# Expert 0's tokens by one-hot products, a joint mask selector, and value products in the array's column halves

## The chip, the cores and the metric

One core of a Trainium2 chip runs one program. The time is the device time of one execution in microseconds (us); the figure compared is the median of the runs. A trace of one execution was taken with the hardware profiler. The engines are TensorE (PE in the rows, with PEld for its weight loads), VectorE (DVE), ScalarE (ACT), GpSimd (POOL) and SyncE (SP), which issues the large transfers.

## The reference

Two transformer blocks on 512 tokens of 1024 columns, in fp32. What matters here:

```python
# first block, SSD mixer: 4 groups of 3 heads, chunks of 128 tokens
lmat = exp(where(causal, a_cs[..., :, None] - a_cs[..., None, :], -inf))
y_diag = einsum('bcgls,bcghls,bcsghp->bclghp', cb, lmat, xdt)
# second block, forgetting attention: 8 heads of 64, query blocks of 128
logits = q @ k.T / sqrt(d) + (cum[t] - cum[s]);  p = softmax(masked logits)
o = p @ v                      # then rms_norm per head
# second block, mixture of experts: 16 experts, two per token
h = h + concat(o_a, o_b) @ w_out
t = rms_norm(h, ffn_norm)
gates = ...                    # top-1 group, top-2 experts in it
for e in range(16):
    y += gates[:, e] * ((silu(t @ w_gate[e]) * (t @ w_up[e])) @ w_down[e])
out = rms_norm(h + y, final_norm)
```

## The kernel before

A scheduler places the instructions of the whole program on the engines; waits come from its semaphores, `issue_after` adds an order by hand. All weights stream from HBM by SP's queue in units of 512 KB (`fill`, line 212, tile `raw`), are split into a high part on ScalarE (`whi`, line 270) and a low part on VectorE, or by a plan on GpSimd (`wlo`, line 271), and go into rings of five. `mm3` (lines 276 to 278) multiplies hi by hi, lo by hi and hi by lo: three matmuls of 512 columns for a product of fp32 quality. A plain fp32 matmul runs as two passes, which the trace shows as two instructions.

*SSD mask.* For each of 4 chunks and 4 groups one unit (`ssd_mask_unit`) makes three heads' differences of cumulative sums in PSUM: the causal mask (line 840), then a selector times the sums' high part (841) and low part (842), 48 partitions each, then the group's products (843).

*Forgetting attention.* For each query block tt and head: q by k (1532), mask (1533), row maximum, exp on ScalarE (1536), transposes of p (`tr`, 1540), a copy `fox_pT` (1543 or 1545), the value product with pT stationary and v's 64 columns moving (1548), and a scale by the row sum's reciprocal on VectorE (1550). Other matmuls of projections fill the gaps.

*Start of the MoE.* The last projection (`projR` over `w_out_2`) adds its result to x per token tile tt (line 403) and calls `after(tt)`: transposes of x (`tr`, 2023), routing logits (2028), the normed rows to HBM (`xnd`), ranks by matmuls (1731, 1732) and a one-hot of expert 0's slots (`rt_oh`, 2049). Once the last tile's rank is known, `slots_row` (1833 to 1841) makes the row numbers of the 96 slots of experts 0 and 1, two indirect transfers on POOL's queue fetch these tokens from `xnd` (`ex_g`, 1874), PE transposes them (1887), and `put_split` (315) makes `ex_xh` and `ex_xl`, the moving side of expert 0's gate and up products. Later experts' rows come from `route`, whose small operations VectorE does at this start. A 4-byte-per-slot transfer `mark` on SP's queue (2116) holds back the weight loads behind it until the row numbers of expert 0 exist. The final norm's gain is brought as one row and spread over the partitions by PE (125, 126).

Of the kernel before, what the change touches and what calls it, by code (L numbers as in the profile page):

```python
# [70 lines left out]
class Kern:  # L71
# [306 lines left out]
    def projR(s, src, ld, nk, get, x, after, tail=3, mid=None, lag=2, order=None):  # L378
# [4 lines left out]
        for half in range(2):  # L383
            cs = slice(half * 512, half * 512 + 512)
# [391 lines left out]
    def ssd_dt(s, pd, x):  # L776
# [725 lines left out]
    def fox_main(s, pool, qa, ka, v, on):  # L1502
# [21 lines left out]
        for tt in range(NT):  # L1524
# [5 lines left out]
            for h in range(8):  # L1530
                ps = s.psm.tile([P, 512], F32, name="sm")
                nc.tensor.matmul(ps[:, :n], qa[:, h, sl], ka[:, h, :n], start=True, stop=False)  # L1532
                nc.tensor.matmul(ps[:, tt * P:n], s.identb, s.neg_gt, start=False, stop=True)
                V.tensor_reduce(nm[:, h:h + 1], ps[:, :n], AX.X, OP.max, negate=True)
                p = pool.tile([P, T], F32, name="fox_p", bufs=2)
                nc.scalar.activation(p[:, :n], ps[:, :n], AF.Exp, bias=nm[:, h:h + 1], accum_out=sm[:, h:h + 1])
                yield
                pt = s.ptr.tile([P, 512], F32, name="tr")
                for j in range(tt + 1):
                    nc.tensor.transpose(pt[:, j * P:j * P + P], p[:, j * P:j * P + P], s.ident)  # L1540
                pT = pool.tile([P, T], F32, name="fox_pT", bufs=2)
                if h % 2:
                    V.tensor_copy(pT[:, :n], pt[:, :n])
# [436 lines left out]
    def moe(s, mixT):  # L1980
# [70 lines left out]
        def after(tt):  # L2051
# [276 lines left out]
```

## Time and profile before

| | us |
|---|---|
| median of 3 runs | 1455.51 (1454.84 to 1457.64) |
| the profiled execution | 1453.98 |
| its span in the trace | 1452.2 |
| TensorE busy in it | 1399.7 |

The span runs from the first to the last instruction of the trace; the profiled execution's own time is 1.8 us longer. Mean granted clock of TensorE is 0.987 of full speed.

### The profile page before, as it was taken

Reading aid. Unit: us, or ns where it says so; the run is one execution under the profiler, and the core shown is the slowest. Engines: PE = TensorE matmul, PEld = TensorE weight load, DVE = VectorE, ACT = ScalarE, POOL = GpSimd, SP = SyncE. Lnnn points to the kernel's source line nnn. Section 1 sums busy time; section 2 is a strip of 40 time slices with the busy share of each in tenths; the row PEclk is TensorE's granted clock in tenths of the full one; section 3 lists DMA queues with packets and bytes.
Section 4 is the critical chain, followed back from the end, with each engine's and each line's share of the span. In section 5 each row is a group of like instructions: output and inputs, shape, how many; then the busy total and the mean of one; then the engine's idle time right before and its main releaser. Section 6 shows DMA issues by size and latency. Waiting matters only on the chain.

```text
span 1452.2 us, 20178 instructions
## 1 busy us (share of the span) xinstructions
PE 1399.7 (96%) x7467; PEld 1130.2 (78%) x7467; DVE 977.7 (67%) x1772; ACT 779.2 (54%) x1200; POOL 103.8 (7%) x103
## 2 busy tenths in 40 slices
PE   7999999999999999999999999999998599999996
PEld 6888887787879888888888889877887367777774
DVE  6989577565465444444365997766555599999997
ACT  6465654434334333233344685554443388888885
POOL 1000000010010000000000400000102111111111
PEclk9999999999999999999999999999999699999998
DMA  7353342521223333323232423120754899999993
GB/s 199 92 136 112 90 131 73 174 88 58 75 71 116 102 95 94 101 88 100 89 101 87 134 74 88 41 77 18 260 204 172 226 357 356 353 343 349 349 349 130
DMA packets 145933, 223.51 MB, mean 154 GB/s; under 512 B 18466, under 2 KB 71106, under 8 KB 145816
## 3 DMA queue, kind: packets, MB, share of 16 engines
q1 hardware_dynamic: 136852, 200.48, 42.7%
q0 software_dynamic: 3568, 10.34, 3.0%
q10 hardware_dynamic: 5412, 11.37, 2.2%
q8 instruction: 59, 0.97, 0.3%
q14 instruction: 42, 0.34, 0.1%
HBM read 208.41 MB, written 14.95 MB: 154 GB/s over the span
## 4 chain that ended last, share of the span: by engine, by line
PE 86%; DVE 6%; ACT 3%; DMA 2%; issue 2%; POOL 1%; DVEq 0%; SPq 0%; ACTq 0%; POOLq 0%
PE mm L276 24%; PE mm L278 24%; PE mm L277 24%; PE sm L1416 2%; PE tr L1548 1%; PE tr L323 1%; PE tr L1887 1%; PE sm L1532 1%; POOL rs_r L291 1%; DMA ex_g<-xnd,sn_i 1%; DVE wlo L271 1%; PE sm L879 1%; PE sm L276 1%; PE tr L1540 1%; PE sm L2028 1%
## 5 line engine op out<-in xcount | busy, mean ns | idle before, releaser
L271 DVE TENSOR_TENSOR wlo<-raw,whi 128x1024 fp32r<-128x1024 f32 (+1 forms) x351 | 423.6, 1222 | 216.4 <-ACT whi L270 213.5
L270 ACT ACTIVATE whi<-raw 128x1024 fp32r<-128x1024 f32 (+1 forms) x356 | 372.7, 1057 | 293.2 <-PE mm L277 154.0
L276 PE MATMUL mm<-hT_hi,whi 128*128 128x512 f32 (+1 forms) x768 | 283.2, 369 | 1.9 <-DVE x L403 1.7
L278 PE MATMUL mm<-hT_hi,wlo 128*128 128x512 f32 (+1 forms) x768 | 281.5, 367 | 0.0
L277 PE MATMUL mm<-hT_lo,whi 128*128 128x512 f32 (+1 forms) x768 | 280.9, 366 | 0.0
L276 PE MATMUL mm<-whi,hT_hi 128*128 128x512 f32 (+1 forms) x592 | 219.7, 371 | 1.4 <-ACT hT_hi L315 1.4
L278 PE MATMUL mm<-whi,hT_lo 128*128 128x512 f32 (+1 forms) x592 | 217.9, 368 | 0.0
L277 PE MATMUL mm<-wlo,hT_hi 128*128 128x512 f32 (+1 forms) x592 | 217.0, 367 | 0.0
L278 PEld LDWEIGHTS mm<-hT_hi,wlo 128*128 128x128 f32 x768 | 144.7, 188 | 24.3
L276 PEld LDWEIGHTS mm<-hT_hi,whi 128*128 128x128 f32 x768 | 144.3, 188 | 24.8 <-DVE x L403 1.9
L277 PEld LDWEIGHTS mm<-hT_lo,whi 128*128 128x128 f32 x768 | 144.6, 188 | 23.3
L276 PEld LDWEIGHTS mm<-whi,hT_hi 128*128 128x128 f32 x592 | 111.8, 189 | 20.7 <-ACT hT_hi L315 2.3
L278 PEld LDWEIGHTS mm<-whi,hT_lo 128*128 128x128 f32 x592 | 111.7, 189 | 19.2 <-issue 0.6
L277 PEld LDWEIGHTS mm<-wlo,hT_hi 128*128 128x128 f32 x592 | 112.0, 189 | 18.5 <-issue 1.0
L276 PE MATMUL mm<-whi,ex_xh 128*96 128x512 f32 x256 | 102.8, 402 | 1.3 <-ACT ex_xh L315 0.6
L291 POOL TENSOR_TENSOR rs_r<-rs_v,mhalf 128x1 f32<-128x1 f32 (+2 forms) x42 | 33.4, 798 | 980.2 <-DVE rs_v L289 823.9
L277 PE MATMUL mm<-wlo,ex_xh 128*96 128x512 f32 x256 | 101.4, 396 | 0.0
L278 PE MATMUL mm<-whi,ex_xl 128*96 128x512 f32 x256 | 100.9, 395 | 0.0
L276 PEld LDWEIGHTS mm<-whi,ex_xh 128*96 128x96 f32 x256 | 41.5, 162 | 19.0 <-ACT ex_xh L315 1.1
L278 PEld LDWEIGHTS mm<-whi,ex_xl 128*96 128x96 f32 x256 | 41.6, 162 | 18.1
L277 PEld LDWEIGHTS mm<-wlo,ex_xh 128*96 128x96 f32 x256 | 41.8, 163 | 16.9
L1246 DVE SCALAR_TENSOR_TENSOR cv<-mm,cols,cv 128x511 f32<-128x511 f32 (+1 forms) x44 | 33.0, 749 | 30.0 <-ACT cv L1243 29.2
(568 smaller groups left out, 2060.3 us busy)
## 6 DMA issues: line engine op xcount, KB each, us to landing
raw<-in_w_gate SPq DMA_DIRECT2D x64, 512.0 KB
raw<-in_w_up SPq DMA_DIRECT2D x64, 512.0 KB
raw<-in_w_down SPq DMA_DIRECT2D x64, 512.0 KB
raw<-in_ffn_w_up SPq DMA_DIRECT2D x44, 512.0 KB
raw<-in_w_in SPq DMA_DIRECT2D x40, 512.0 KB
raw<-in_ffn_w_down SPq DMA_DIRECT2D x22, 512.0 KB
raw<-in_w_out SPq DMA_DIRECT2D x16, 512.0 KB
raw<-in_w_in SPq DMA_DIRECT2D x8, 520.0 KB
```

The costliest lines, as they stand in the source:

```text
L270: s.hi_op = s.nc.scalar.activation(hv, v, AF.Copy).ins
L271: eng.tensor_sub(lv, v, hv.bitcast(F32))
L276: mm(ps, a.hi[asl], b.hi[bsl], start=first, stop=False)
L277: mm(ps, a.hi[asl], b.lo[bsl], start=False, stop=False)
L278: mm(ps, a.lo[asl], b.hi[bsl], start=False, stop=last)
L291: s.pow_op = nc.gpsimd.tensor_tensor(r, v, s.mhalf[:, :n], OP.pow).ins
L323: nc.tensor.transpose(ps[:, i * P:(i + 1) * P], src[:, (k0 + i) * P:(k0 + i + 1) * P], s.ident)
L879: nc.tensor.matmul(yd[:, o:o + 64], L[:, j], xdt[:, h], start=True, stop=True)
L1246: V.scalar_tensor_tensor(y[:, d:], ps[:, :512 - d], cw[:, w:w + 1], y[:, d:], op0=OP.mult, op1=OP.add)
L1416: nc.tensor.matmul(ps[:, sl], qk[:, sl], qk[:, sl], start=True, stop=True)
L1532: nc.tensor.matmul(ps[:, :n], qa[:, h, sl], ka[:, h, :n], start=True, stop=False)
L1540: nc.tensor.transpose(pt[:, j * P:j * P + P], p[:, j * P:j * P + P], s.ident)
```

## The change

Three parts. (1) The SSD mask's sums are stacked, high parts in partitions 0 to 47 and low parts in 64 to 111, so that one matmul over 128 partitions stands where two over 48 stood; the stacking takes a memset and copies once. (2) In the forgetting attention v is stationary (128 by 64) and pT moves 128 columns; two heads' results go to PSUM partitions 0 to 63 and 64 to 127. The pair is copied by ScalarE (`fox_oT`), transposed back by PE and scaled by one VectorE operation. (3) Expert 0's tokens are not fetched: `first(tt)` multiplies chunks of x (stationary) by a one-hot (now fp32, `rt_oh0`) into two PSUM tiles, and 8 ScalarE and 8 VectorE operations make `ex_xh` and `ex_xl` with the norm's gain. `mark` and expert 0's gather go; two early splits move from GpSimd to VectorE; the final gain comes as one 512 KB transfer on POOL's queue; expert 1's row numbers are made on VectorE alone, and its transposes are ordered after the third unit of expert 0's up product.

```diff
--- before
+++ after
@@ -381,6 +381,7 @@
+            adds = s.add_ops = []
@@ -400,7 +401,7 @@
-                nc.vector.tensor_add(x[:, tt, cs], x[:, tt, cs], pss[tt])
+                adds.append(nc.vector.tensor_add(x[:, tt, cs], x[:, tt, cs], pss[tt]).ins)
@@ -806,26 +807,34 @@
...
+        c2 = s.tmp.tile([P, P], F32, name="ssd_c2", tag="h")
+        V.memset(c2, 0.0)
+        for r in (0, 64):
+            V.tensor_copy(c2[:, r:r + 48], cs[:, 0].rearrange("p a b -> p (a b)"))
         pt = s.ptr.tile([P, 512], F32, name="tr")
-        nc.tensor.transpose(pt[:48, 0:P], cs[:, 0].rearrange("p a b -> p (a b)"), s.ident)
-        hl = s.tmp.tile([48, 2, P], F32R, name="ssd_hl", tag="h")
-        hi, lo = hl[:, 0], hl[:, 1]
-        s.put_split(pt[:48, 0:P], hi, lo)
-        s.ssd_cs = Split(*(pd.tile([48, 3, P], F32R, name="ssd_c" + i) for i in ("H", "L")))
-        sh = [48, 3, P]
-        for o, v in ((s.ssd_cs.hi, hi), (s.ssd_cs.lo, lo)):
-            V.tensor_mul(o, v.bitcast(F32)[:, None, :].to_broadcast(sh), hm[:, :, None].to_broadcast(sh))
+        nc.tensor.transpose(pt[:, 0:P], c2, s.ident)
+        hl = s.tmp.tile([P, 2, P], F32R, name="ssd_hl", tag="h")
+        nc.scalar.activation(hl[:, 0], pt[:, 0:P], AF.Copy)
+        V.tensor_sub(hl[:, 1], pt[:, 0:P], hl[:, 0].bitcast(F32))
+        s.ssd_cs = pd.tile([P, 3, P], F32R, name="ssd_cH")
+        sh = [64, 3, P]
+        for i in range(2):
+            r = slice(64 * i, 64 * i + 64)
+            V.tensor_mul(s.ssd_cs[r], hl[r, i].bitcast(F32)[:, None, :].to_broadcast(sh), hm[r, :, None].to_broadcast(sh))
         yield
@@ -836,10 +845,9 @@
-        sel = s.ssd_sel[:, u:u + 1].to_broadcast([48, P])
...
-        nc.tensor.matmul(o, sel, s.ssd_cs.hi.rearrange("p j t -> p (j t)"), start=False, stop=False)
-        nc.tensor.matmul(o, sel, s.ssd_cs.lo.rearrange("p j t -> p (j t)"), start=False, stop=True)
+        nc.tensor.matmul(o, s.ssd_sel[:, u:u + 1].to_broadcast([P, P]), s.ssd_cs.rearrange("p j t -> p (j t)"),
+                         start=False, stop=True)
@@ -1527,27 +1535,40 @@
-            for h in range(8):
...
+            for h0 in range(0, 8, 2):
+                pTs = []
+                for h in (h0, h0 + 1):
...
+                    yield
+                    pt = s.ptr.tile([P, 512], F32, name="tr")
...
+                    pTs.append(pT)
+                V.reciprocal(ri[:, h0:h0 + 2], sm[:, h0:h0 + 2])
+                for j in range(tt + 1):
+                    for i in range(2):
+                        nc.tensor.matmul(pt[i * 64:i * 64 + 64, 0:P], v[:, j, (h0 + i) * 64:(h0 + i) * 64 + 64],
+                                         pTs[i][:, j * P:j * P + P], start=j == 0, stop=j == tt)
+                oT = pool.tile([P, P], F32, name="fox_oT", bufs=2)
+                nc.scalar.activation(oT, pt[:, 0:P], AF.Copy)
+                next(rest, None)
                 yield
-                pt = s.ptr.tile([P, 512], F32, name="tr")
...
-                V.reciprocal(ri[:, h:h + 1], sm[:, h:h + 1])
-                for j in range(tt + 1):
-                    nc.tensor.matmul(pt[:, 0:64], pT[:, j * P:j * P + P], v[:, j, h * 64:h * 64 + 64],
-                                     start=j == 0, stop=j == tt)
-                V.tensor_scalar_mul(on[:, tt, h * 64:h * 64 + 64], pt[:, 0:64], ri[:, h:h + 1])
+                nc.tensor.transpose(pt[:, P:2 * P], oT, s.ident)
+                hs = slice(h0 * 64, h0 * 64 + P)
+                V.tensor_mul(on[:, tt, hs].rearrange("p (h d) -> p h d", h=2),
+                             pt[:, P:2 * P].rearrange("p (h d) -> p h d", h=2),
+                             ri[:, h0:h0 + 2, None].to_broadcast([P, 2, 64]))
                 next(rest, None)
@@ -1795,8 +1816,9 @@
-        V.tensor_tensor(oh, s.slot[:, None, :].to_broadcast([P, 8, CAP]),
-                        rk.rearrange("p i t -> p (i t)")[:, :, None].to_broadcast([P, 8, CAP]), OP.is_equal)
+        with s.tc.issue_after(s.row_op):
+            V.tensor_tensor(oh, s.slot[:, None, :].to_broadcast([P, 8, CAP]),
+                            rk.rearrange("p i t -> p (i t)")[:, :, None].to_broadcast([P, 8, CAP]), OP.is_equal)
@@ -1833,12 +1855,8 @@
         ix = pool.tile([CAP, 1], I32, name=f"sn_i{e}")
-        if e:
-            nc.scalar.activation(v, ps[:CAP, 0:2], AF.Copy)
-        else:
-            nc.vector.tensor_copy(v, ps[:CAP, 0:2])
-        eng = nc.gpsimd if e else nc.vector
-        s.row_op = eng.tensor_scalar(ix, v[:, 0:1], v[:, 1:2], float(T), op0=OP.add, op1=OP.add).ins
+        nc.vector.tensor_copy(v, ps[:CAP, 0:2])
+        s.row_op = nc.vector.tensor_scalar(ix, v[:, 0:1], v[:, 1:2], float(T), op0=OP.add, op1=OP.add).ins
         return ix
@@ -1894,12 +1912,17 @@
             for k in range(2):
-                s.mm3(ps[:CAP], xT, (slice(None), k0 + k), w, (slice(None), k), k0 + k == 0, k0 + k == 7)
+                op = s.mm3(ps[:CAP], xT, (slice(None), k0 + k), w, (slice(None), k), k0 + k == 0, k0 + k == 7)
+            if k0 == 4:
+                s.gate_op = op
         return ps
+    def expert_xT(s, pool):
+        return Split(pool.tile([P, KD, CAP], F32R, name="ex_xh", bufs=1),
+                     pool.tile([P, KD, CAP], F32R, name="ex_xl", bufs=1))
     def expert_pick(s, pool, xg):
-        xT = Split(pool.tile([P, KD, CAP], F32R, name="ex_xh", bufs=1),
-                   pool.tile([P, KD, CAP], F32R, name="ex_xl", bufs=1))
+        xT = s.expert_xT(pool)
         s.pick(xg, lambda k0, ps: s.put_split(ps, xT.hi[:, k0:k0 + 4], xT.lo[:, k0:k0 + 4]))
@@ -2013,7 +2036,16 @@
         s.rr = pr.tile([P, NT], F32, name="rt_r")
-        oh = pr.tile([P, NT, CAP], BF16, name="rt_oh")
+        oh = [pr.tile([P, NT, CAP], (F32, BF16)[e], name=f"rt_oh{e}") for e in range(2)]
+        p0 = []
+        def first(tt):
+            for b in range(2):
+                for k in range(4):
+                    c = (4 * b + k) * P
+                    nc.tensor.matmul(p0[b][:, k * CAP:(k + 1) * CAP], x[:, tt, c:c + P], oh[0][:, tt],
+                                     start=tt == 0 and k == 0, stop=tt == 3 and k == 3)
@@ -2046,7 +2078,8 @@
             s.route_rank(tt, pl[:, 160 + tt * 16:176 + tt * 16])
-            V.tensor_scalar(oh[:, tt], s.slot, s.rk[:, tt, 0:1], None, op0=OP.is_equal)
+            for e in range(2):
+                V.tensor_scalar(oh[e][:, tt], s.slot, s.rk[:, tt, e:e + 1], None, op0=OP.is_equal)
@@ -2058,6 +2091,10 @@
                     ranks(tt - 1)
+            if tt == 3:
+                p0.extend(s.pmm.tile([P, 512], F32, name="mm") for _ in range(2))
+                for i in range(3):
+                    first(i)
             V.scalar_tensor_tensor(la[:, tt], pl[:, tt * 20:tt * 20 + 20], r, s.rb, op0=OP.mult, op1=OP.add)
@@ -2074,7 +2111,11 @@
         s.projR("w_out_2", D, KD, lambda half, k: mixT, x, after, mid=mid, lag=0, order=(4, 6, 0, 2), tail=3)
+        gf = s.gain.tile([P, D], F32, name="gain")
+        with s.tc.issue_after(s.pow_op):
+            nc.gpsimd.dma_start(gf, dap(A["final_norm_2"], 0, [[0, P], [1, D]]))
         ranks(3)
+        first(3)
@@ -2084,39 +2125,30 @@
-        hi_op = None
-        s.plan = [(nc.gpsimd, []), (nc.gpsimd, [s.pow_op])]
+        s.plan = [(V, [s.add_ops[0]]), (V, [s.add_ops[1]])]
+        late, s.late = s.late, 1000
         s.fill(most=L3, splits=2)
-        hi_op = s.hi_op
+        s.late = late
-        ix = []
-        for e in range(XG):
-            if e:
-                oh = pn.tile([P, NT, CAP], BF16, name="sn_oh")
-                sh = [P, NT, CAP]
-                V.tensor_tensor(oh, s.slot[:, None, :].to_broadcast(sh), s.rk[:, :, e:e + 1].to_broadcast(sh), OP.is_equal)
-            with s.tc.issue_after(s.rank_op):
-                ix.append(s.slots_row(pn, e, oh))
-            s.gather(xgs[e], ix[e])
-            if not e:
-                s.fence = [s.row_op]
-        grow = s.tmp.tile([1, D], F32, name="grow", tag="h", bufs=1)
-        with s.tc.issue_after(hi_op):
-            nc.scalar.dma_start(grow, dap(A["final_norm_2"], 0, [[D, 1], [1, D]]))
-        with s.tc.issue_after(s.logit_op), s.tc.issue_after(hi_op):
-            gf = s.bcast_pe(s.gain, grow, "gain")
+        with s.tc.issue_after(s.rank_op):
+            ix1 = s.slots_row(pn, 1, oh[1])
+        s.gather(xgs[1], ix1)
         for tt in range(AL, NT):
...
         s.rings["raw"] = [s.pool(f"raw4_{i}", ctx=c3, side="right") for i in range(N4)] + s.rings["raw"]
-        mark = s.dram.tile([CAP, 1], I32, name="mark")
-        with s.tc.issue_after(nc.sync.dma_start(mark, ix[0]).ins):
-            s.fill()
+        s.fence = [s.row_op]
+        s.fill()
         s.late = FL[5]
-        xT = s.expert_pick(pe, xgs[0])
+        xT = s.expert_xT(pe)
+        for k in range(KD):
+            ps = p0[k // 4][:, k % 4 * CAP:k % 4 * CAP + CAP]
+            gk = s.cols2[:, 96 + k:97 + k]
+            nc.scalar.activation(xT.hi[:, k], ps, AF.Copy, scale=gk)
+            V.scalar_tensor_tensor(xT.lo[:, k], ps, gk, xT.hi[:, k].bitcast(F32), op0=OP.mult, op1=OP.subtract)
         s.route(pr, pe, lgg, lge)
@@ -2159,7 +2191,8 @@
             pu = s.expert_gate(pe, e, xT, "w_up_2")
-            xT = s.expert_pick(pe, xgs[(e + 1) % XG])
+            with s.tc.issue_after(s.gate_op) if e == 0 else nullcontext():
+                xT = s.expert_pick(pe, xgs[(e + 1) % XG])
             if e:
```

On TensorE, from the last tile's transposes on, these rows stood ahead of expert 0 before (`rt_o` a matrix of ones, `grow` the final gain's row, `ex_g_9992` expert 0's tokens, `ex_xh` and `whi` the first expert product):

```order
L1748 LDWEIGHTS rt_o
L1748 MATMUL sm<-rt_Mb,rt_o 128x16
L125 MATMUL mm<-grow,ones 128x512 x2
L1887 MATMUL tr<-ident,ex_g_9992 128x96 x8
L276 MATMUL mm<-whi,ex_xh 96x512
L277 MATMUL mm<-wlo,ex_xh 96x512
L276 MATMUL mm<-whi,ex_xh 96x512
```

In the changed kernel the products of `first` begin right behind the projection's last matmuls, on both sides of the last tile's transposes (2055 is the old line 2023, 2060 the old 2028):

```order
L277 MATMUL mm<-wlo,hT_hi 128x512
L278 MATMUL mm<-whi,hT_lo 128x512
L2047 MATMUL mm<-rt_oh_9484,x 128x96 x15
L2055 MATMUL tr<-ident,x 128x128 x4
L2047 MATMUL mm<-rt_oh_9484,x 128x96
L2060 MATMUL sm<-rt_w,rt_h 128x20 x4
L1752 LDWEIGHTS rt_o
```

The last eight of `first` stand directly ahead of expert 0, with the small matmuls of expert 1's row numbers (1855):

```order
L1769 MATMUL sm<-rt_Mb,rt_o 128x16
L2047 MATMUL mm<-rt_oh_9484,x 128x96 x8
L1855 LDWEIGHTS rt_oh_9485
L1855 MATMUL sm<-rt_tb,rt_oh_9485 96x2
L276 MATMUL mm<-whi,ex_xh 96x512
L277 MATMUL mm<-wlo,ex_xh 96x512
L278 MATMUL mm<-whi,ex_xl 96x512
```

So expert 0 now stands behind `first(3)` and not behind a transfer, line 125 is gone, and 15 products of `first` stand ahead of the last tile's transposes. Expert 1's eight transposes stand after all of expert 0's gate and up products, as before.

On VectorE, before, this piece of the route's work ended ahead of expert 0's two `ex_xl`:

```order
L271 TENSOR_TENSOR wlo<-raw,whi 128x1024
L1772 TENSOR_TENSOR rt_M_10146<-rt_M,rt_w 128x128
L1782 TENSOR_TENSOR rt_y_10148<-rt_tb,rt_M 128x64x2
L1784 TENSOR_TENSOR rt_y_10148<-rt_M,rt_r 128x64
L1782 TENSOR_TENSOR rt_y_10148<-rt_tb,rt_M 128x64x2
L1784 TENSOR_TENSOR rt_y_10148<-rt_M,rt_r 128x64
L1786 COPY rt_y_10148<-rt_M_10146 128x128
L1798 TENSOR_TENSOR rt_y_10149<-rt_s,rt_rk_10159 128x768
L315 TENSOR_TENSOR ex_xl<-tr,ex_xh 128x384 x2
```

In the changed kernel the same stretch has eight smaller `ex_xl` mixed with the route's operations and a weight split (`wlo`):

```order
L2151 SCALAR_TENSOR_TENSOR ex_xl<-mm,cols_2799,ex_xh 128x96 x2
L1789 TENSOR_TENSOR rt_w<-rt_w,rt_se 128x4
L1818 TENSOR_REDUCE rt_rk_10181<-rt_x 128x4
L2151 SCALAR_TENSOR_TENSOR ex_xl<-mm,cols_2799,ex_xh 128x96 x2
L1790 RECIPROCAL rt_w<-rt_w 128x4
L1817 TENSOR_TENSOR rt_x<-rt_M,rt_rk 128x64
L1791 TENSOR_TENSOR rt_w<-rt_w,rt_e_10155 128x4
L271 TENSOR_TENSOR wlo<-raw,whi 128x1024
L2151 SCALAR_TENSOR_TENSOR ex_xl<-mm,cols_2799,ex_xh 128x96 x2
L1793 TENSOR_TENSOR rt_M_10168<-rt_M,rt_w 128x128
```

What stood ahead of expert 0's splits now stands among and behind them.

In the attention's last query block, TensorE before (`fox_v` and `fox_pT` in the value product, each of four rows two passes):

```order
L1540 MATMUL tr<-ident,fox_p 128x128 x4
L277 MATMUL mm<-wlo,hT_hi 128x512
L278 MATMUL mm<-whi,hT_lo 128x512
L1540 MATMUL tr<-ident,fox_p 128x128 x4
L1548 MATMUL tr<-fox_v,fox_pT 128x64 x4
L276 MATMUL mm<-whi,hT_hi 128x512
L277 MATMUL mm<-wlo,hT_hi 128x512
```

and in the changed kernel, where two heads' products stand in one row and the transpose of `fox_oT` follows behind two matmuls of a projection:

```order
L1561 MATMUL tr<-fox_pT,fox_v 64x128 x8
L276 MATMUL mm<-whi,hT_hi 128x512
L277 MATMUL mm<-wlo,hT_hi 128x512
L1567 MATMUL tr<-ident,fox_oT 128x128
L1550 MATMUL tr<-ident,fox_p 128x128 x4
L1542 MATMUL sm<-fox_k,fox_q 128x512
L1550 MATMUL tr<-ident,fox_p 128x128 x4
```

Two value products of 64 columns became a pair of 128 columns, with one transpose more for the pair.

## Rows read from the trace of the kernel before

**Rows 1.** Page, part 4: the chain that ended last, by engine
```profile
PE 86%; DVE 6%; ACT 3%; DMA 2%; issue 2%; POOL 1%; DVEq 0%; SPq 0%; ACTq 0%; POOLq 0%
```

**Rows 2.** Stretches: length; busy us of PE, PEld, DVE, ACT, POOL; PEclk, DMA share, GB/s
```profile
955.00:1025.00 70.00, 69.26 (x414) 52.71 (x413) 42.88 (x132) 32.55 (x83) 6.59 (x4) 1.00 0.16 46
...
1130.00:1146.60 16.60, 5.57 (x20) 2.67 (x18) 5.21 (x24) 3.00 (x6) 3.42 (x3) 0.50 0.92 165
1146.60:1161.20 14.60, 13.95 (x67) 9.53 (x66) 10.31 (x19) 9.97 (x12) 1.79 (x2) 0.90 0.85 287
1180.00:1280.00 100.00, 100.00 (x476) 70.99 (x475) 91.99 (x91) 86.11 (x102) 14.56 (x11) 1.00 1.04 356
1410.00:1420.00 10.00, 10.00 (x47) 7.04 (x46) 8.91 (x9) 8.72 (x10) 1.57 (x1) 1.00 0.73 234
```

**Rows 3.** Timeline of PE at the MoE's start: start, us, operation, idle before
```profile
1121.43 0.66 PE L2023 MATMUL tr<-ident,x 128*128 128x128 f32 x4 [2.54 <-DVE x L403]
...
1129.23 0.24 PE L1833 MATMUL sm<-rt_tb,rt_oh 128*96 128x2 bf16 x1 [0.34 <-DVE rt_oh L2049]
...
1145.10 1.54 PE L1887 MATMUL tr<-ident,ex_g 96*128 96x96 f32 x8 [11.03 <-DMA ex_g<-xnd,sn_i]
1146.62 0.74 PE L276 MATMUL mm<-whi,ex_xh 128*96 128x512 f32 x1
```

**Rows 4.** The chain over the same stretch: start, us
```profile
1118.70 1.75 DVE rt_oh L2049
...
1124.87 1.32 DVE rs_t L301
1130.83 14.23 DMA ex_g<-xnd,sn_i
```

**Rows 5.** Timeline of VectorE: the same one-hot later, and the last splits
```profile
1128.92 0.26 DVE L2049 TENSOR_SCALAR rt_oh<-rt_s,rt_rk 128x96 bf16<-128x96 f32 x1
...
1429.06 2.36 DVE L271 TENSOR_TENSOR wlo<-raw,whi 128x1024 fp32r<-128x1024 f32 x2 [0.20 <-ACT whi L270]
```

**Rows 6.** Timeline of POOL: a weight split
```profile
1118.03 2.35 POOL L271 TENSOR_TENSOR wlo<-raw,whi 128x1024 fp32r<-128x1024 f32 x1 [1.13 <-ACT whi L270]
```

**Rows 7.** Timeline of PE: one SSD mask unit
```profile
184.20 0.43 PE L841 MATMUL sm<-ssd_cH,ssd_sel 48*128 48x384 f32 x1
184.48 0.34 PE L842 MATMUL sm<-ssd_cL,ssd_sel 48*128 48x384 f32 x1
```

**Rows 8.** Timeline of PE in the forgetting attention
```profile
1000.11 0.60 PE L1540 MATMUL tr<-ident,fox_p 128*128 128x128 f32 x4
1000.55 1.02 PE L1532 MATMUL sm<-fox_k,fox_q 66*128 66x512 f32 x2
1001.46 1.10 PE L1548 MATMUL tr<-fox_v,fox_pT 128*128 128x64 f32 x8
1002.40 0.22 PE L1533 MATMUL sm<-neg_gt,identb 128*128 128x128 bf16 x1
```

**Rows 9.** Lines 1548 and 1545 over the span: ns min/median/max, first and last start
```profile
L1548 PE MATMUL tr<-fox_v,fox_pT x160: 217/275/323, 949.0 to 1020.1; 128*128 128x64 f32 x160
...
L1545 ACT ACTIVATE fox_pT<-tr x16: 277/428/598, 948.7 to 1017.2; 128x128 f32<-128x128 f32 x4, 128x256 f32<-128x256 f32 x4, 128x384 f32<-128x384 f32 x4, 128x512 f32<-128x512 f32 x4
```

**Rows 10.** Timeline of PE: S5's products in the array's column halves
```profile
105.39 0.39 PE L277 MATMUL mm<-hT_lo,whi 128*128 128x512 f32 x1
105.63 0.40 PE L278 MATMUL mm<-hT_hi,wlo 128*128 128x512 f32 x1
105.95 2.09 PE L686 MATMUL sm<-s_U,s_I 128*64 128x64 f32 x64
107.97 0.55 PE L695 MATMUL sm<-s_U,s_T 128*128 128x64 f32 x3
```

**Rows 11.** Tile ex_g: its gathers from issue to landing
```profile
DMA to landing us min/median/max: 8.4/11.4/14.4
```

**Rows 12.** Page, part 5: ScalarE's weight splits, mean ns of one
```profile
L270 ACT ACTIVATE whi<-raw 128x1024 fp32r<-128x1024 f32 (+1 forms) x356 | 372.7, 1057 | 293.2 <-PE mm L277 154.0
```

More of the change, by code (lines that the diff above doesn't have):

```diff
@@ L277, in mm3 @@
         mm(ps, a.hi[asl], b.lo[bsl], start=False, stop=False)
-        mm(ps, a.lo[asl], b.hi[bsl], start=False, stop=last)
+        return mm(ps, a.lo[asl], b.hi[bsl], start=False, stop=last).ins
     def rstd(s, ss, n, width, pool, v0=None, out=None):
@@ L807, in ssd_dt @@
         yield
-        it = s.tmp.tile([48, 16], F32, name="ssd_it", tag="h")
-        nc.gpsimd.iota(it, pattern=[[-3, 16]], base=0, channel_multiplier=1, allow_small_or_imprecise_dtypes=True)
-        eq = s.tmp.tile([48, 4, 16], F32, name="ssd_eq", tag="h")
+        it = s.tmp.tile([P, 16], F32, name="ssd_it", tag="h")
+        for r in (0, 64):
+            nc.gpsimd.iota(it[r:r + 64], pattern=[[-3, 16]], base=0, channel_multiplier=1,
+                           allow_small_or_imprecise_dtypes=True)
+        eq = s.tmp.tile([P, 4, 16], F32, name="ssd_eq", tag="h")
         for j in range(3):
@@ L1529, in fox_main @@
             ri = s.stat.tile([P, 8], F32, name="fox_ri")
-            for h in range(8):
[L1531 to L1536, printed above, removed]
-                yield
-                pt = s.ptr.tile([P, 512], F32, name="tr")
-                for j in range(tt + 1):
[L1540 to L1543, printed above, removed]
-                else:
-                    nc.scalar.activation(pT[:, :n], pt[:, :n], AF.Copy)
-                V.reciprocal(ri[:, h:h + 1], sm[:, h:h + 1])
-                for j in range(tt + 1):
-                    nc.tensor.matmul(pt[:, 0:64], pT[:, j * P:j * P + P], v[:, j, h * 64:h * 64 + 64],
-                                     start=j == 0, stop=j == tt)
-                V.tensor_scalar_mul(on[:, tt, h * 64:h * 64 + 64], pt[:, 0:64], ri[:, h:h + 1])
@@ new lines, in fox_main @@
+            for h0 in range(0, 8, 2):
+                pTs = []
+                for h in (h0, h0 + 1):
+                    ps = s.psm.tile([P, 512], F32, name="sm")
+                    nc.tensor.matmul(ps[:, :n], qa[:, h, sl], ka[:, h, :n], start=True, stop=False)
+                    nc.tensor.matmul(ps[:, tt * P:n], s.identb, s.neg_gt, start=False, stop=True)
+                    V.tensor_reduce(nm[:, h:h + 1], ps[:, :n], AX.X, OP.max, negate=True)
+                    p = pool.tile([P, T], F32, name="fox_p", bufs=2)
+                    nc.scalar.activation(p[:, :n], ps[:, :n], AF.Exp, bias=nm[:, h:h + 1], accum_out=sm[:, h:h + 1])
+                    yield
+                    pt = s.ptr.tile([P, 512], F32, name="tr")
+                    for j in range(tt + 1):
+                        nc.tensor.transpose(pt[:, j * P:j * P + P], p[:, j * P:j * P + P], s.ident)
+                    pT = pool.tile([P, T], F32, name="fox_pT", bufs=3)
+                    if h % 2:
+                        V.tensor_copy(pT[:, :n], pt[:, :n])
+                    else:
+                        nc.scalar.activation(pT[:, :n], pt[:, :n], AF.Copy)
+                    pTs.append(pT)
+                V.reciprocal(ri[:, h0:h0 + 2], sm[:, h0:h0 + 2])
+                for j in range(tt + 1):
+                    for i in range(2):
[4 more added lines that the diff above has]
+                next(rest, None)
+                yield
+                nc.tensor.transpose(pt[:, P:2 * P], oT, s.ident)
[3 more added lines that the diff above has]
+                             ri[:, h0:h0 + 2, None].to_broadcast([P, 2, 64]))
```

6 lines of the change are left out of this document (3 added, 3 removed).

## The prediction

> **What bounds the kernel now.** I read the chain that ended last first: TensorE holds 86% of it [rows 1]. Then the stretches [rows 2]: in the attention's, 955 to 1025, TensorE is busy 69.3 of 70 us, and among the experts, 1180 to 1280, 100 of 100. There an instruction taken off TensorE is worth its slot, from its start to the next one's, and work added on other engines costs nothing until one of them is full. VectorE is near that among the experts (92 of 100 us), and the DMA engines too (share 1.04, 356 GB/s). The one large hole is the MoE's start: between 1130 and 1146.6 TensorE does 5.6 us of work. Its timeline shows why [rows 3]: a wait of 2.54 us for the last tile of x, the last one-hot used at 1129.23, and then 11.03 us of idling until expert 0's tokens land; the first expert product starts at 1146.62. The chain names three pieces there [rows 4]: a one-hot of 1.75 us, a small operation of 1.32 us, the transfer of 14.23 us. The clock granted is 0.50, the lower level, from 1130 to 1146.6, and 0.90 on the mean of the next 14.6 us [rows 2]: after idling the engine works at half speed for a while, and 0.10 of 14.6 us is 1.5 us lost.
>
> **SSD mask.** Line 841 takes .28 us, to the start of line 842 [rows 7], which is of the same form. One matmul of the same 384 columns over 128 partitions replaces both. How long it takes over more partitions no row shows for this form; a 512-column product over 128 partitions takes .24 to the next one [rows 10], so nothing speaks for more than .28. One slot of some .27 goes, in 16 units: −4.3 us. The stacking's memset and two copies are some .5 us of VectorE work, once, in a mixer that TensorE fills; if bare, +.5.
>
> **Value products.** 8 passes took 1001.46 to 1002.40, .1175 each [rows 8]; there are 160 [rows 9], so 18.8 us. The new form also has 160 passes (80 products, two each), each of 128 columns over half the array, the halves in turn. The nearest row is S5's: 64 passes of 64 columns into column halves took 105.95 to 107.97, .0316 each [rows 10]; twice the columns gives .063, 10.1 us in all. If the halves did not overlap, a pass of 128 columns would take what a transpose of 128 does, .44 / 4 = .11 [rows 8], 17.6 in all. I take .063, since that row has this very form of output. To it come 16 transposes of `fox_oT` at .11, 1.8 us. Going into the halves cost .09 there (.32 for the product ahead against .24 for the one before), coming out I put at .11; at 16 pairs 3.2 us. And the new path, value product, ScalarE copy, transpose, needs cover: ScalarE's copy of 128 columns takes .28 us [rows 9], with the two hand-overs I estimate .6, and the new order puts two to five other matmuls of .23 us in between, .46 us and up. In half the pairs I count .1 to .2 us bare, 1 us in all. Sum: −18.8 + 10.1 + 1.8 + 3.2 + 1 = −2.7; as some of the old waits already lay in the 18.8, I take −2. Bounds −6 (no price for the halves, all covered) and +5 (halves not overlapped).
>
> The Trainium skill, TensorEngine Tiling (Array Packing), section Key Properties, says that a change of tiling mode drains TensorE, which speaks against this part. The product ahead of S5's row has .40 us of duration and left after .32 [rows 10], so what stands there is no full drain; were each of 32 changes a drain at .40 − .24 = .16 us, it would be 5.1 us in place of 3.2, and this part would come to about 0.
>
> **Start of the MoE.** Where the last one-hot was used at 1129.23 [rows 3], the changed order gives: the one-hot that holds the chain for 1.75 us [rows 4] while GpSimd splits a weight (1118.03 for 2.35 us [rows 6]) takes .26 elsewhere [rows 5], −1.5; the 1.32 us operation on a column of 128 values [rows 4], which should take no more than that either, −1.1; the last tile's transposes stand behind 15 products of `first`, of two passes each at about .1175 [rows 8], 3.5 us from 1118.7, when the 2.54 us wait began, so they start at 1122.2 and not 1121.43 [rows 3], +.75; two splits that move to VectorE (2.36 us for two [rows 5]), mostly in a pause, +.5. Together the last one-hot at about 1127.9. `first(3)` is 8 × .23 = 1.85 us, a ScalarE copy of a quarter tile .3: expert 0 starts at about 1130.0 and not at 1146.62, −16.6. If TensorE stays at full clock there (it has 7.4 us of new products in the old pauses), −1.5 as well. The matmuls of line 125, last ahead of expert 0's transposes, lay under the gather's wait and give nothing more.
>
> Against it stands VectorE's work, for which the wait was the cover. From 1130 to 1161.2, when expert 1 starts, it did 5.21 + 10.31 = 15.5 us [rows 2]: route, `ex_xl`, weight splits. TensorE's work on expert 0 is 48 products of .23 to .24 and some small ones, 11.5 us. Queued behind the route's operations on VectorE are the splits of up's units, for which TensorE waits. So VectorE is 4.0 us too late, at most; with 8 small `ex_xl` for 2 large ones about as much is added as the new order does earlier. I take the whole 4.0, since nothing else then limits. Sum −16.6 − 1.5 + 4.0 = −14. Bounds: −18 (VectorE keeps up: the splits ahead in the ring suffice) and −8 (expert 1 late too, below).
>
> **The sum** is −4.3 − 2 − 14 = −20.3 against the profiled execution's 1453.98, so 1433.7; the median lies 1.5 above that execution, so **1435**.
>
> **The rivals.**
> *Expert 1's tokens are late* (0.10). Its gather is issued after `first(3)`, at about 1131.2, and gathers took 8.4 to 14.4 us to land [rows 11]: 1139.6 to 1145.6. Expert 1 wants them at 1141.5, or 1145.5 if VectorE is late. For it: the weight loads that `mark` held back (165 GB/s in 1130 to 1146.6 against 356 later [rows 2]) now run beside it. Against it: later gathers ran beside the full stream, and only one now stands where two did. Price 3 to 6 us more: 1438 to 1441.
> The Trainium skill, SBUF — State Buffer, section SBUF: two separate sides, says that a transfer issued from GpSimd cannot write its descriptors while VectorE holds their shared port; VectorE will be full when this one is issued. The range of landings above already includes those with VectorE at 92%.
>
> *The weight stream becomes the bound* (0.10). TensorE gains 14 us here, the stream only what its hole gives: (1 − 165/356) × 16.6 = 8.9 us at most, less 1.4 for the 512 KB of the final gain. Its margin at the end: the transfers end near 1417 (share .73 of 1410 to 1420 [rows 2]), the last two splits begin at 1429.06 [rows 5], with 1.06 of ScalarE's part ahead [rows 12] some 11 us of margin. 14 − 7.5 = 6.5 would be eaten, 4.5 left. If the hole does not close, 14 eats all of it and 3 us more: 1438.
>
> *More than I sum* (0.13). VectorE is hidden (−4) or the attention's part reaches its bound (−4): 1427 to 1431.
>
> *Slower* (0.04). The attention's pair path is bare: TensorE waits in each of 16 pairs until ScalarE, behind one weight split of 1.06 us [rows 12] and another operation of that kind, copies `fox_oT`. It decides above (20.3 − 1) / 16 = 1.2 us bare in each pair beside what I counted; with two operations ahead, 2.1 + .6 − .5 of cover = 2.2 us, it is +34 against −20, and 1469 or so; with one ahead, 1.2, no change. Against it: ScalarE is busy 32.6 of 70 us there [rows 2], so it is free more often than not when the pair ends.
>
> *The change does not do what it says* (0.03): another wait of the start takes the gather's place (the 8 ScalarE and VectorE operations, or `first(3)`, behind late splits), and the attention eats the mask's gain: 1453 to 1457.
>
> **How the numbers follow.** My forecast, 1429 to 1441, has 0.60. With the late gather, the stream and part of the larger gain the range 1427 to 1445 leaves out the rest, under 2 in 10. A change of 0.2%, 2.9 us, is about what a measurement of this kernel tells from none. Faster: 0.60 + 0.10 + 0.10 + 0.13 = 0.93; within 0.2%: 0.03; slower: 0.04.
>
> **What would show it.** Right: the slot of the joint selector at .24 to .28 and one a unit; pairs of value passes at .06 each and little idling ahead of the `fox_oT` transposes; expert 0's first product some 17 us nearer to the last product of w_out, at full clock; TensorE idling 3 to 5 us within expert 0 and before expert 1, for `wlo` or `ex_xl`. Wrong: passes at .11; waits for `fox_oT` over .5 us in most pairs; expert 1's transposes waiting for `ex_g`; waits for `raw` near the end.

## The result and the profile after

The changed kernel takes 1431.21 us (median of 4, 1429.26 to 1432.94) against 1455.32: ratio 0.9831, 95% interval 0.9813 to 0.9849, 24.1 us faster. 1435 was forecast, in 1427 to 1445. The profiled execution took 1432.94, the slowest of the four; its span is 1431.2, 21.0 below that of before. Where these went, from the starts of TensorE's first or last product of each kind in the two traces:

| from, to | before | after | change |
|---|---|---|---|
| start, first mask unit | 173.75 | 174.88 | +1.1 |
| first mask unit, cross attention's first product (SSD) | 147.83 | 138.81 | −9.0 |
| to the attention's first `fox_q` product | 622.12 | 623.58 | +1.5 |
| to the first `hg_v` product behind the attention | 80.49 | 78.57 | −1.9 |
| to the last product of w_out | 94.31 | 94.28 | 0.0 |
| to expert 0's first product | 28.12 | 13.91 | −14.2 |
| to expert 0's first down product (`ex_hh`) | 27.60 | 28.57 | +1.0 |
| to the end | 277.98 | 278.60 | +.6 |

The rows of untouched code move as much between executions that share that code: the first took 173.75 to 175.43 us in four (before, e7, e3, e4; the stacking is not in them), the third 622.1 to 623.6 us in the same four. The +.6 at the end stands in every kernel with the new start (278.5 to 278.6 us against 277.9 to 278.1); where it comes from stays open.

One mask unit, first of before (the two lines of [rows 7] stand between these), then of after:

```profile
183.94 0.33 PE L840 MATMUL sm<-neg_lt,identb 128*128 128x384 bf16 x1
...
184.99 0.36 PE L276 MATMUL mm<-memT_hi,whi 128*128 128x256 f32 x1
```

```profile
183.96 0.33 PE L848 MATMUL sm<-neg_lt,identb 128*128 128x384 bf16 x1
183.98 0.48 PE L849 MATMUL sm<-ssd_cH,ssd_sel 128*128 128x384 f32 x1
184.30 0.38 PE L851 MATMUL sm<-CT,BT 128*128 128x128 f32 x2
184.44 0.36 PE L277 MATMUL mm<-memT_lo,whi 128*128 128x256 f32 x1
```

To the next product it took 1.05 us, now .48. All 16 units are alike, 1.045 us on the mean before and .481 after. That is .57 off in place of the .27 that I counted: besides the second selector product, the rows around it shrank. The mask ahead of the selector (840, now 848) went from .26 to .03 to the next start, and the group's products (843, now 851) from .25 to .14.

In the attention, one group of the last query block, and what TensorE waited for over the stage (us in total, times, longest):

```profile
994.97 1.09 PE L1561 MATMUL tr<-fox_pT,fox_v 128*64 128x128 f32 x16
996.00 0.23 PE L1543 MATMUL sm<-neg_gt,identb 128*128 128x128 bf16 x1
```

```profile
PE tr L1561 <- DVE fox_pT L1553: 1.7, 3, 0.6
PE tr L1567 <- ACT fox_oT L1564: 1.0, 1, 1.0
```

16 passes take 1.03 us to the start of the next product, .064 each; over the stage 160 passes take 11.2 us where 17.3 stood. The shorter groups are dearer by the pass: groups of 4, 8, 12 and 16 take .37, .59, .81 and 1.03 us, which is .055 a pass and .15 for each group. The groups of before have no such part (8 passes .81 to .94, .117 a pass by a line through all groups). Waits went from .6 to 2.7 us.

The MoE's start, the timeline of TensorE and the stretches (columns as in [rows 2]):

```profile
1110.35 3.48 PE L2047 MATMUL mm<-rt_oh,x 128*128 128x96 f32 x30
1113.67 0.60 PE L2055 MATMUL tr<-ident,x 128*128 128x128 f32 x4
...
1116.69 3.07 PE L2047 MATMUL mm<-rt_oh,x 128*128 128x96 f32 x16 [0.60 <-DVE rt_oh L2082]
...
1120.44 3.73 PE L2047 MATMUL mm<-rt_oh,x 128*128 128x96 f32 x16
...
1124.03 0.72 PE L276 MATMUL mm<-whi,ex_xh 128*96 128x512 f32 x1
...
1128.69 0.47 PE L276 MATMUL mm<-whi,ex_xh 128*96 128x512 f32 x1 [0.46 <-ACT ex_xh L2150]
...
1138.05 0.82 PE L1905 MATMUL tr<-ident,ex_g 96*128 96x96 f32 x8
1140.35 0.47 PE L276 MATMUL mm<-whi,ex_xh 128*96 128x512 f32 x1 [1.48 <-ACT ex_xh L315]
```

```profile
1110.12:1124.03 13.91, 12.72 (x93) 12.25 (x92) 9.35 (x57) 4.20 (x8) 1.15 (x2) 0.76 1.01 350
1124.03:1127.60 3.57, 3.57 (x11) 2.37 (x10) 3.08 (x14) 1.39 (x5) 1.06 (x1) 0.50 0.90 297
1127.60:1141.00 13.40, 11.46 (x61) 7.63 (x59) 11.90 (x29) 11.02 (x15) 4.16 (x1) 1.00 1.00 341
1160.00:1360.00 200.00, 200.00 (x950) 142.00 (x949) 184.00 (x180) 171.93 (x204) 29.29 (x23) 1.00 1.04 352
```

Expert 0 starts 13.9 us behind w_out where it was 28.1. No wait there names VectorE beyond the .60 for a one-hot, nor the gather of expert 1. But the granted clock is 0.50, the lower level, from 1117.4, within the first stretch, to 1127.7: `first(2)` and `first(3)`, of 16 passes each, take 2.87 and 3.52 us to the next row, the 30 passes ahead 3.32. Before expert 1 the wait is 1.48 for `ex_xh`. From 1160 on TensorE is gapless as before, and TensorE never waits for the weight stream, at 352 GB/s.

The profiled execution of a second measurement of the same kernel (e0_after, below) has a span of 1428.6 us, with 13.6 us to expert 0 and 27.5 from there to `ex_hh`: there the clock was at 0.50 for 6.8 us of this start, here for 10.2.

### The profile page after: what moved, and what is told of

Its sections match the earlier page's. It is cut to its first block, busy times and chain, and to the rows that moved or that the text cites. A ratio compares the mean times of both kernels' runs of the same rounds, so it can differ in the third digit from the quotient of the medians.

```text
span 1431.2 us, 20262 instructions
## 1 busy us (share of the span) xinstructions
PE 1393.5 (97%) x7515; PEld 1129.9 (79%) x7515; DVE 972.1 (68%) x1754; ACT 779.1 (54%) x1218; POOL 98.9 (7%) x101
## 4 chain that ended last, share of the span: by engine, by line
PE 71%; DVE 3%; ACT 1%; issue 1%; POOL 1%; DMA 0%; DVEq 0%; POOLq 0%; ACTq 0%; SPq 0%
PE mm L276 20%; PE mm L278 20%; PE mm L277 20%; PE sm L1424 2%; PE tr L1905 1%; PE sm L1542 1%; POOL rs_r L291 1%; PE mm L2047 1%; PE sm L276 1%; PE tr L1561 1%; PE sm L278 1%; PE tr L323 1%; PE sm L277 1%; PE sm L2060 0%; PE tr L1550 0%
## 5 line engine op out<-in xcount | busy, mean ns | idle before, releaser
L278 PEld LDWEIGHTS mm<-whi,hT_lo 128*128 128x128 f32 x592 | 112.3, 190 | 18.8 <-issue 0.8
```

Source lines behind the costliest of these rows:

```text
L278: return mm(ps, a.lo[asl], b.hi[bsl], start=False, stop=last).ins
```

## The experiments

All ratios are to the kernel before.

**e1_ssd, e3_fox, e4_moe: each part alone**, the other hunks of the diff left out.

> Only the joint mask selector, the rest as before. If the matmul's own slot is what it saves (my prediction's term): 16 x .27 = 4.3 us off 1455.3, 1451.0. If going from products over 128 partitions to products over 48 and back costs about .2 us each way, which the joint selector removes too: 16 x (.17 + .2 + .2) less some .08 that the next product gives back, 6 to 8 us off, 1447.5 to 1449.5.

Measured: 1447.60, ratio 0.9943 (0.9930 to 0.9956), −8.3 us. The second case of its expectation, steps between 128 and 48 partitions.

> Only the attention's value products in the column halves, the rest as before. My prediction's term: -2 us, 1453.3. If the attention alone is worth nothing (passes cheaper, but steps into and out of the halves, transposes and waits eat it): 1455.3 within 1 us. The profile should show passes of about .07 and the product behind each group of them some .1 us later than elsewhere.

Measured: 1453.06, ratio 0.9983 (0.9974 to 0.9991), −2.5 us by the ratio: my term, and clear of no change, though only by a little.

> Only the start of the MoE by one-hot products, the rest as before. My prediction's term: -14 us, 1441.3. From the changed kernel's trace, where the offset to before goes from -8.4 at the last projection's end to -21.2 in the experts: -12.8, 1442.5. If the three parts help each other (the start finds other buffers free than alone): less than 12, over 1443.5.

Measured: 1442.84, ratio 0.9909 (0.9896 to 0.9922), −13.2 us. The three ratios multiply to 0.9836; the parts add up, and no help of one to another shows.

**e2_ssd_two: is it the number of selector products, or their 48 partitions?** On e1:

```diff
-        nc.tensor.matmul(o, s.ssd_sel[:, u:u + 1].to_broadcast([P, P]), s.ssd_cs.rearrange("p j t -> p (j t)"),
-                         start=False, stop=True)
+        for r in range(2):
+            nc.tensor.matmul(o, s.ssd_sel[:, r, u:u + 1].to_broadcast([P, P]), s.ssd_cs.rearrange("p j t -> p (j t)"),
+                             start=False, stop=r == 1)
```

> The stacked sums of the joint selector, but still two selector matmuls a unit, each over all 128 partitions with a selector that is zero in the other half. If a matmul's slot is the cost: no change to before, 1455 (+.5 for the added VectorE work). If the step between 48 and 128 partitions is the cost: the two slots shrink to about .17 each and the steps are gone, 16 x .4 less .08 x 16 is some 4 to 5 us off, 1450 to 1452, and the mask ahead of them takes .03 instead of .26 start to start.

Measured: 1449.89, ratio 0.9960 (0.9948 to 0.9973), −5.8 us with as many products as before. Its timeline of TensorE, one unit:

```profile
188.09 0.33 PE L851 MATMUL sm<-neg_lt,identb 128*128 128x384 bf16 x1
188.12 0.65 PE L853 MATMUL sm<-ssd_cH,ssd_sel 128*128 128x384 f32 x2
188.60 0.38 PE L855 MATMUL sm<-CT,BT 128*128 128x128 f32 x2
188.74 0.36 PE L277 MATMUL mm<-memT_lo,whi 128*128 128x256 f32 x1
```

.65 to the next product: .40 less than before's 1.05, with the mask at .03 and two selector products in .48; the 16 units are alike, .654 on the mean. So two steps between 128 and 48 partitions cost .40 us a unit, 6.4 in 16 units, and the second product the rest, .17 a unit. The Trainium skill, TensorEngine Tiling (Array Packing), section Key Properties, says that a change of tiling mode drains TensorE; these rows agree with it if a product over 48 partitions counts as such a change, which no run here shows by itself. I had not looked for it in this part of the change. For the column halves the rows show .15 us a group (above and e11).

**e5_fox_serial: do the halves have to alternate?** The loop over the pair's two heads stands outside that over j.

> The changed kernel (1431.2), with the value products of a pair in the order first all of one head, then all of the other, so that the column halves no longer alternate. If the halves overlap only when they alternate: the passes go from .07 to about .11, 160 x .04 = 6.4 us more, 1437 to 1438. If half an array's columns are cheaper in any order: .07 as before, 1431.

Measured: 1433.46, ratio 0.9837 (0.9823 to 0.9852), by its time not separable from the changed kernel. Its timeline, the same group as above:

```profile
996.03 1.58 PE L1561 MATMUL tr<-fox_pT,fox_v 128*64 128x128 f32 x16
997.54 0.23 PE L1543 MATMUL sm<-neg_gt,identb 128*128 128x128 bf16 x1
```

1.51 us for 16 passes, .094 each, against .064: here alternating saves a third. But groups of 4 and 8 take .37 and .59 us in either order; only those of 12 and 16 are longer, by .27 and .49 us. So the order counts where six or eight passes of one half stand in a row, and not where two or four do. Over the stage the passes take 14.2 us for 11.2, the stage 80.8 us for 78.6. Neither number of the expectation: a pass in one half alone is not the .11 of a whole array's 128 columns.

**e6_fox_wide: no column halves.** Per j one product with both heads' v stationary, 128 columns, and both pT moving:

```diff
-                    for i in range(2):
-                        nc.tensor.matmul(pt[i * 64:i * 64 + 64, 0:P], v[:, j, (h0 + i) * 64:(h0 + i) * 64 + 64],
-                                         pTs[i][:, j * P:j * P + P], start=j == 0, stop=j == tt)
...
+                    nc.tensor.matmul(pt[:, 0:2 * P], v[:, j, h0 * 64:h0 * 64 + P], pT[:, j].rearrange("p i t -> p (i t)"),
+                                     start=j == 0, stop=j == tt)
...
+                nc.scalar.activation(oT[0:64], pt[0:64, 0:P], AF.Copy)
+                nc.scalar.activation(oT[64:P], pt[64:P, P:2 * P], AF.Copy)
```

> The changed kernel, with the value products over the whole array: v of both heads is stationary (128 columns), the pT of both move as 256 columns, and of the 128 x 256 results the two blocks that are wanted are copied, in two ScalarE operations. Passes: 80 of 256 columns, which at the rate of the 512-column products of q and k (.44) take .22, 17.7 us against 11.2. If stepping into and out of the column halves costs some .28 us a pair, as the products behind the pairs show (.31 against .26 three in a row): +6.5 -4.5, 1433. If it costs nothing: 1437 to 1438.

Measured: 1441.24, ratio 0.9899 (0.9884 to 0.9914), 10 us over the changed kernel: neither. The passes are 17.3 us as worked out (+6.1). The waits:

```profile
PE tr L1559 <- DVE fox_pT L1553: 1.8, 2, 1.1
PE tr L1550 <- ACT fox_p L1546: 1.5, 1, 1.5
PE tr L1566 <- ACT fox_oT L1563: 1.5, 3, 1.1
```

4.7 us for 2.7. The stage is 88.0 us for 78.6, so some 1.3 us beyond passes and waits are not placed. What it does say: the passes over the whole array are dearer than those in the halves with their .15 a group, and beside the passes no price of the halves came back.

**e11_fox4: half as many groups.** Four heads' value products in a row, one copy of 256 columns, two transposes, one scale for four heads; pT in four buffers.

> The changed kernel, with the value products of four heads together, so 8 groups in the halves in place of 16, 8 ScalarE copies and 8 VectorE scales fewer. If stepping into and out of the halves costs some .28 us a group: 8 x .28 = 2.2 us off, 1429, and no waits on fox_oT that were not there. If it costs nothing, or the longer way to the values leaves TensorE waiting: 1431 or more.

Measured: 1432.16, ratio 0.9834 (0.9821 to 0.9848): no gain in the time. The stage is 78.3 us for 78.6. Its passes and waits:

```profile
1007.79 1.97 PE L1563 MATMUL tr<-fox_pT,fox_v 128*64 128x128 f32 x32
1009.69 0.51 PE L276 MATMUL mm<-whi,hT_hi 128*128 128x512 f32 x1
```

```profile
PE tr L1550 <- ACT fox_p L1546: 2.3, 3, 0.9
PE tr L1570 <- ACT fox_oT L1566: 1.0, 1, 1.0
```

32 passes take 1.90 us, where two groups of 16 take 2.05, and over the stage the passes take 9.9 us for 11.2: 1.2 us less with 8 groups fewer, again .15 a group. So each group in the halves has a price, about half of the .28 asked for, and this run shows where it went: .6 us more of waits in the stage, and 1.3 us more behind it, where a projection waits 1.6 us for ScalarE's `hT_hi` in place of .3. Both branches of the expectation hold in part. Beside the .15 no price shows: the .31 us products behind a group, from which I read .28, stand behind any product of another kind too, as behind the transpose of `fox_oT` at 996.59 in the changed kernel (.32).

**e7_no_mark: the kernel before without `mark`.**

```diff
-        mark = s.dram.tile([CAP, 1], I32, name="mark")
-        with s.tc.issue_after(nc.sync.dma_start(mark, ix[0]).ins):
-            s.fill()
+        s.fill()
```

> The kernel before without the small transfer that holds back the weight loads; expert 0's tokens are gathered as before. If the gather was slow because it is a transfer behind other transfers (the changed kernel's one for expert 1 landed within 10.6 us beside the full weight stream): it lands some 4 to 6 us earlier or as late as before, and the time is 1450 to 1455. If the small transfer itself is what kept the transfer engines from work (46 GB/s behind it): at 8 us after its issue, 6 us off, 1449. If it protected the gather: later than 14 us, 1456 and more.

Measured: 1450.90, ratio 0.9958 (0.9944 to 0.9972), −6.1 us. POOL's row with the issue of expert 0's gather, TensorE's wait for it, and the stretch:

```profile
1133.90 1.11 POOL L1874 DMA_INDIRECT ex_g<-xnd,sn_i  x1 [4.64 <-DMA raw<-in_w_up]
```

```profile
1141.55 1.54 PE L1887 MATMUL tr<-ident,ex_g 96*128 96x96 f32 x8 [4.41 <-DMA ex_g<-xnd,sn_i]
```

```profile
1133.00:1141.50 8.50, 4.14 (x12) 1.50 (x11) 5.28 (x25) 2.51 (x5) 3.42 (x3) 0.50 1.04 356
```

From its issue to the transposes that wait for it, expert 0's gather takes 7.6 us beside a stream of 356 GB/s, where behind `mark` it took 14.23 [rows 4] at 165 GB/s [rows 2]. Expert 1's, the second, lands after 8.8 us; in the four kernels that have `mark` and both gathers (before, e1, e2, e3) it took 13.3 to 14.5. So it was not the weight stream that delayed the gather, but the small transfer or what it makes of the queue; which of the two stays open. 6 of the 13 us of the MoE's part were to be had by leaving `mark` out, without one-hot products.

**e8_pool_splits: the two early splits on GpSimd again.**

```diff
-        s.plan = [(V, [s.add_ops[0]]), (V, [s.add_ops[1]])]
+        s.plan = [(nc.gpsimd, []), (nc.gpsimd, [s.pow_op])]
```

> The changed kernel (1431.2), with the two early weight splits again on GpSimd instead of VectorE. My prediction counts -1.5 and -1.1 for small VectorE operations that no longer run beside a GpSimd split and +.5 for the two splits: undone, +2 us, 1433. If the last tile's chain has slack elsewhere (the products of the second and third tile stand in front of it): within .7 us, 1431 to 1432.

Measured: 1434.07, ratio 0.9853 (0.9834 to 0.9872), 3 us over the changed kernel by the medians, within the intervals of each other; expert 0 starts 16.4 us behind w_out for 13.9. One of two such pairs there, VectorE's longest operation and POOL's split:

```profile
1116.44 2.29 DVE L301 SCALAR_TENSOR_TENSOR rs_t<-rs_r,rs_h 128x1 f32<-128x1 f32 x1 [0.49 <-POOL rs_r L291]
```

```profile
1116.37 2.35 POOL L271 TENSOR_TENSOR wlo<-raw,whi 128x1024 fp32r<-128x1024 f32 x1
```

Twice an operation on 128 values, which takes .22 in the changed kernel, ends when the split ends (the other pair 2.31 us beside 2.38). So a collision costs some 2.1 us; the 2.5 us by which expert 0 starts later fit the sum −1.5 − 1.1 + .5. The time does not separate it, and TensorE's order differs too (14 passes of `first` ahead of the last transposes, not 30).

**e9_order: the second tile's one-hot products behind the last transposes.**

```diff
-                for i in range(3):
-                    first(i)
+                first(0)
+                with s.tc.issue_after(s.tr_op):
+                    first(1)
+                first(2)
```

> The changed kernel (1431.2), with the one-hot products of the second tile put behind the last tile's transposes, not ahead of them: the transposes could start at 1112.1 where they started at 1113.67. If the chain of the last tile and the clock set expert 0's start: 1 to 2 us earlier from the chain, and the fuller pauses may hold the clock up, up to 4.5 us more (.9 + 1.7 for the products of the third and fourth tile, 1.8 in expert 0): 1425 to 1430. If VectorE's work is the limit, as my prediction's +4.0 says: the same time, 1431.

Measured: 1431.20, ratio 0.9822 (0.9809 to 0.9836). To this belongs a second measurement of the changed kernel, e0_after:

> The changed kernel once more, beside the next three on the same chip: 1429 to 1433, ratio .983.

Measured: 1430.37, ratio 0.9828 (0.9804 to 0.9852). The new order is not separable from it. In its profiled execution the stage changed as expected. Its stretch, TensorE's timeline, and a row of ScalarE:

```profile
1110.86:1122.65 11.79, 10.00 (x93) 9.45 (x91) 8.31 (x51) 4.04 (x7) 1.15 (x2) 1.00 0.99 343
```

```profile
1119.64 2.02 PE L2047 MATMUL mm<-rt_oh,x 128*128 128x96 f32 x16
...
1122.65 0.47 PE L276 MATMUL mm<-whi,ex_xh 128*96 128x512 f32 x1 [0.99 <-ACT ex_xh L2152]
...
1123.74 0.47 PE L278 MATMUL mm<-whi,ex_xl 128*96 128x512 f32 x1 [0.37 <-DVE sn_v L1858]
```

```profile
1122.26 0.34 ACT L2152 ACTIVATE ex_xh<-mm,cols 128x96 fp32r<-128x96 f32 x1 [3.30 <-DMA xnd<-hl]
```

The clock stays at 1.00, the higher level, `first(3)` takes 1.86 us for 3.52, and expert 0 starts 11.8 us behind w_out for 13.9. Then .99 and .37 us of waits follow, and .68 later: ScalarE's first `ex_xh` waits for the transfer that writes `hl` to HBM.

That the order held the clock up is not shown. The start of e5 is the changed kernel's, product by product, with the same pauses ahead (.49 and .60 us), and there too the clock stayed at 1.00. Its stretch from w_out to expert 0, `first(3)` and expert 0's first product:

```profile
1112.68:1125.05 12.37, 9.99 (x94) 9.40 (x92) 8.25 (x51) 4.11 (x7) 1.15 (x2) 1.00 0.99 343
```

```profile
1121.94 2.02 PE L2047 MATMUL mm<-rt_oh,x 128*128 128x96 f32 x16
...
1125.05 0.48 PE L276 MATMUL mm<-whi,ex_xh 128*96 128x512 f32 x1 [1.08 <-ACT ex_xh L2150]
```

Six profiled executions have the changed kernel's order here. From w_out's last product to `ex_hh` the clock was at 0.50 for 10.2 us (the changed kernel), 6.8 (e0_after, e4, e6), 3.4 (e11) and none (e5), and that way took 42.5, 41.1 to 41.3, 41.6 and 40.4 us. So the order does not settle whether the clock falls; what does stays open. e5 against the changed kernel puts the cost of the fall at 2.1 us, 1.5 of them ahead of expert 0, with more waiting for `ex_xh` in e5 (1.08 us ahead of expert 0, and 1.50 in e11, where the other four have none).

**e13_both: e9 and e11.**

> Four heads together and the second tile's one-hot products behind the last tile's transposes. If both gains stand and add: -2.2 and -2, 1427. If the run before with the order alone moved only within its spread: 1429.

Measured: 1433.87, ratio 0.9843 (0.9829 to 0.9856): a miss, by the medians slower than either alone. TensorE's longest wait in expert 0's start (us in total, times, longest):

```profile
PE mm L276 <- ACT ex_xh L2155: 2.5, 1, 2.5
```

ScalarE's timeline has what `ex_xh` waited for:

```profile
1125.43 0.34 ACT L2155 ACTIVATE ex_xh<-mm,cols 128x96 fp32r<-128x96 f32 x1 [4.83 <-DMA xnd<-hl]
```

It is the same transfer. Behind this wait the clock granted is 0.50, from 1125.8 to 1132.2, in e9's order; and e11's wait of 1.5 us for `hT_hi` stands here too. No version here beats the changed kernel by more than its interval.

## Why the prediction was right, step by step

*SSD mask, −4.3: mis-sized, measured −8.3* (e1). "One slot of some .27 goes" is the term; e2 puts .17 a unit on the product itself and .40 on the two steps between 48 and 128 partitions, which I had counted nowhere. I weighed the rule on changes of tiling mode only against the attention. The mechanism that I gave, a slot that goes, is .17 of the .57 us a unit; the joint selector's own slot is .32, and not .24 to .28.

*Value products, −2: right in sum* (e3 −2.5), by terms that were not all right. The old passes were 17.3 us and not 18.8, since I took the .1175 of one group of eight for all. The new ones came to 11.2, .070 on the mean (.063 taken): .055 a pass, and .15 for each of 16 groups, 2.4 us where I put 3.2 for stepping in and out, and not the 5.1 of a drain at each of 32 changes. For `fox_pT` and `fox_oT` stand 2.1 us more of waiting, where I took 1. With the 1.8 of the transposes that is −2.2; the stage gave −1.9.

*MoE's start, −14: measured −13.2* (e4), with other terms, and that the sum came out is in part luck. −16.6 to expert 0's start was −14.2. "If TensorE stays at full clock there" did not hold in the profiled execution: the two groups of `first` took 1.0 and 1.7 us longer than in e5 (1.87 and 1.86 us, at 1.00), and since the last rank's product stands behind `first(2)`, its loss is on the path. With the clock at 1.00 throughout (e5) it was −15.8, as TensorE then waits 1.08 us for `ex_xh`, beyond the .3 that I had for a copy. The 1.5 us in expert 0 were not won either, not even at 1.00, where e5 waits .38, .68 and 1.46 us in it. Of the 3 to 5 us of idling that I named as a sign, the changed kernel has 1.9, and none for `wlo` or `ex_xl`. "I take the whole 4.0" for VectorE failed: no wait in expert 0 of the changed kernel names it. From expert 0's start to `ex_hh` the stage took 1.0 us more: waits of .46 and 1.48 us for `ex_xh` in place of .65 and .61, and .7 us longer at the lower level. Ahead of the 1.48, before expert 1, ScalarE's table load and `ex_h` stood ahead of `ex_xh`. So a loss that did not come, 4.0, made up for gains that did not come, 2.4 and 1.5. The removed collisions are shown by e8.

*The rivals.* The gather of expert 1 was never waited for: issued at 1125.68, it landed 9.5 us later, and its transposes start at 1138.05 without a wait. TensorE did not wait for the stream. The pair path was bare for 1.0 us once. Nothing here sets the clock's level alone: that its fall costs 2.7 us in the two groups of `first`, and 2.1 over the start, is read from e5's rows beside the changed kernel's.

## What to carry to other kernels

Count a product over few partitions not by its columns alone: look at the rows before and behind it, and at what the same neighbours take where nothing of another partition count stands between them. A fence of 96 tiny writes ahead of a gather cost 6 us here; beside the weight loads that it was to hold back the gather took 7.6 us, behind the fence 14.2 (e7). And when a wait goes, look at the clock of what now fills the place, in more than one execution: the same order of products ran at either level, and one trace of each kernel alone puts the difference down to the order.

## What the runs showed that I had not expected

A mask product of 384 bf16 columns takes .26 us ahead of a 48-partition product and .03 ahead of one over 128 (starts of rows, of which products overlap); a unit of four products 1.05 against .65 with the same count. Groups of products into alternating column halves take .055 us a pass of 128 columns and .15 us a group; in one half after the other 16 passes take 1.51 us for 1.03, but 8 passes the same .59. A gather of 96 rows lands in 8 to 9 us beside 356 GB/s of weights, and in 14 behind a transfer of 96 single words. And one order of products ran its first 14 us behind w_out at either level of the clock.
